# The opening of a two-block layer: partial sums on two engines, product passes outermost, weight rounding ahead of the modulation

## Chip, cores and metric

One core of one Trainium2 chip runs the whole program in one launch. The metric is device time in microseconds (us), the median of several executions; the profile is of one execution.

## The reference, cut to what matters

Two transformer blocks on 256 tokens of 1024 features, in float32. The change touches only the start of the first block:

```python
c_act = silu(c)                                   # (1, 1024)
mod = (c_act @ w_ada + b_ada).reshape(1, 6, 1024) # w_ada: 1024 x 6144
shift1, scale1 = mod[:, 0], mod[:, 1]             # columns 0 to 2047 of w_ada
u = rms_norm(x, ln1) * (1.0 + scale1) + shift1    # (256, 1024)
proj = u @ w_in                                   # only 1536 columns of it in the opening
```

Behind the opening come the rest of `proj`, the convolution and state-space branches, the first MLP, and the whole second block.

## The kernel before

**Precision.** Each float32 product is made of three fp32r products: operands are split into a rounded high part (ScalarE copies to fp32r) and a low part (what the rounding left, a subtraction), and high x high, high x low and low x high are summed in PSUM. For weights the parts are called `wh` and `wl`, for the activations `uh` and `ul`.

**The opening** (lines 386 to 575) stands in a manual schedule: every engine runs its instructions in the order of the program text. It has four pairs p = 0 to 3, each of two blocks k = 2p, 2p+1 of 128 features. The activations `us` are normalised and transposed but not yet modulated. For each pair:

- `load_a0(p)` brings 2 MB of `w_ada` (four transfers on SP's queue, two halves `a0[p,0]`, `a0[p,1]`); `do_load()` brings one block's 0.75 MB of `w_in` into one of four `raw` buffers, which are free again when the weight's low part has been made.
- `acc0(p, h)` on VectorE multiplies the eight 128-row slices by c and adds them up in `ac0` (one tensor_scalar and seven scalar_tensor_tensor of 512 columns per pair).
- `sum0(p)` sums `ac0` over partitions on TensorE (four matmuls with one moving column, each two instructions in the trace), and VectorE makes the scale and shift columns `gs0` (three small instructions).
- `mod0(k)`: ScalarE modulates the 256 tokens of block k in place (line 494) and rounds them to `uh` (495); VectorE makes `ul` (496).
- `split0(k)`: ScalarE rounds the 1536 weight columns to `wh` (lines 503 and 504); the low part is made in three pieces of 512, two on GpSimd and one on VectorE (line 507).
- `prod0(k, u0, u1)`: 36 matmuls of 256 columns per block (6 output tiles x 2 x 3 passes); the six PSUM tiles `first` gather all eight blocks. The three passes of one weight tile follow each other, so `wl` is wanted by the third matmul.

In the loop over k, half of `acc0(p+1)` stands before each block's products on VectorE; `sum0(p+1)` stands in the middle of the odd block's products, followed by `mod0` and `split0` of the next pair. Before the loop SP issues five small vectors (`rc`: c, c_2, ln1, two pieces of b_ada), the two halves of x, pair 0, two weight blocks, pair 1 and two weight blocks. In the loop it issues pair p+2 in the first two pairs, one weight block for each k, and at k = 4 eleven small vectors (`smalls`).

Behind the opening the order is a planner's; weights come through the same `raw`, `wh` and `wl` buffers (four each), and the six `first` tiles are read out there.

Of the kernel before, what the change touches and what calls it, by code (L numbers as in the profile page):

```python
# [8 lines left out]
F32 = mybir.dt.float32  # L9
F32R = mybir.dt.float32r  # L10
AF = mybir.ActivationFunctionType
ALU = mybir.AluOpType
# [25 lines left out]
def tile_hybrid_blocks(ctx: ExitStack, tc: tile.TileContext, a: dict, out: bass.AP, dbg=None):  # L38
    nc = tc.nc
# [13 lines left out]
    act, dve, pool, pe = nc.scalar.activation, nc.vector, nc.gpsimd, nc.tensor  # L53
# [4 lines left out]
    def aux(name):  # L58
        return ps_aux.tile([128, 512], F32, tag="aux", name=name)

    cur = {}
# [149 lines left out]
    tri3 = const.tile([128, 3, 128], F32, name="tri3")  # L211
# [174 lines left out]
    NS = 6  # L386
    start = ExitStack()
    start.enter_context(tc.manual_schedule())
    ph = phase("start")
    rc = cur["p"].tile([40, 128], F32, tag="rc", name="rc")  # L390
    for i, src in enumerate((a["c"][0], a["c_2"][0], a["ln1"][0], a["b_ada"][0, 0:1024], a["b_ada"][0, 1024:2048])):
        nc.sync.dma_start(rc[8 * i : 8 * i + 8], src.rearrange("(r q) -> r q", q=128))
    x0 = cur["p"].tile([128, 2, D], F32, tag="xtok", name="x0")
    for t in range(2):
        nc.sync.dma_start(x0[:, t, :], a["x"][0, t * 128 : (t + 1) * 128, :])
# [1 line left out]
    a0 = {}  # L397

    def load_a0(p):

        for h in range(2):
# [5 lines left out]
    smalls, later_smalls = [], []  # L407
    r1 = cur["p"].tile([96, 128], F32, tag="r1", name="r1")
    rows = [("ln2", a["ln2"][0], 8), ("ln1g2", a["ln1_g_2"][0], 8), ("ln2g2", a["ln2_g_2"][0], 8),
            ("cw", a["conv_w"][0].rearrange("t c -> (t c)"), 24), ("nw", a["ssm_norm_w"][0], 16), ("cbias", a["ssm_conv_b"][0], 32)]  # L410
    base = 0
    at_row = {}
    for nm, ap, n in rows:
        smalls.append((r1[base : base + n], ap.rearrange("(r q) -> r q", q=128)))
        at_row[nm] = base
        base += n
    r2 = cur["p"].tile([128, 128], F32, tag="r2", name="r2")
    smalls.append((r2, a["ssm_conv_w"][0].rearrange("t c -> (t c)").rearrange("(r q) -> r q", q=128)))
    wdt = const.tile([128, 8, 32], F32, name="wdt")
# [33 lines left out]
    dve.scalar_tensor_tensor(ccol, cth, 1.0, csb[:, :16], op0=ALU.add, op1=ALU.mult)  # L453
    dve.tensor_scalar(ccol, ccol, 0.5, None, op0=ALU.mult)
    ada_c.append(ccol)
    bsc = const.tile([128, 8], F32, name="bsc")
    dve.tensor_scalar(bsc, csb[:, 32:40], 1.0, None, op0=ALU.add)
    lncol, bsh = csb[:, 16:24], csb[:, 24:32]
# [3 lines left out]
    gs0 = const.tile([128, 2, 8], F32, name="gs0")  # L462
    ac0 = {}

    def acc0(p, h):
        v = a0.pop((p, h))
        if h == 0:
            ac0[p] = cur["p"].tile([128, 2, 256], F32, tag="ac0", name="ac0", bufs=2)
        t = ac0[p]
        for ko in range(4):  # L470
            c = ccol[:, 4 * h + ko : 4 * h + ko + 1]
            if h == 0 and ko == 0:
                dve.tensor_scalar(t, v[:, ko], c, None, op0=ALU.mult)
            else:
                dve.scalar_tensor_tensor(t, v[:, ko], c, t, op0=ALU.mult, op1=ALU.add)

    def sum0(p):
        t = ac0.pop(p)
        ps = aux("adaps")
        for s_ in range(2):  # L480
            for j in range(2):
                pe.matmul(ps[:, 2 * s_ + j : 2 * s_ + j + 1], t[:, s_, 128 * j : 128 * j + 128], ones32[:, 0:1],
                          start=True, stop=True)
        ks = slice(2 * p, 2 * p + 2)
        dve.tensor_tensor(gs0[:, 0, ks], ps[:, 0:2], bsh[:, ks], op=ALU.add)
        for j in range(2):
            k = 2 * p + j
            dve.scalar_tensor_tensor(gs0[:, 1, k : k + 1], ps[:, 2 + j : 3 + j], bsc[:, k : k + 1], lncol[:, k : k + 1],
                                     op0=ALU.add, op1=ALU.mult)

    def mod0(k):
        p, j = k // 2, k % 2
        f = us[p][:, j, :]
        act(f, f, AF.Identity, scale=gs0[:, 1, k : k + 1], bias=gs0[:, 0, k : k + 1])
        act(uh[p][:, j, :], f, AF.Copy)
        dve.tensor_tensor(ul[p][:, j, :], f, uh[p][:, j, :].bitcast(F32), op=ALU.subtract)

    def split0(k):

        v = raws.pop(k)  # L500
        wh, wl = (w_p.tile([128, 2048], F32R, tag=n_, name=n_, bufs=4)[:, :1536].rearrange("p (k n) -> p k n", k=3)
                  for n_ in ("wh", "wl"))
        act(wh[:, 0:1, :], v[:, 0:1, :], AF.Copy)
        act(wh[:, 1:3, :], v[:, 1:3, :], AF.Copy)  # L504
        for q in (1, 2, 0):
            e_ = dve if q == 2 else pool
            e_.tensor_tensor(wl[:, q, :], v[:, q, :], wh[:, q, :].bitcast(F32), op=ALU.subtract)  # L507
        splits[k] = (wh, wl)
        st["split"] += 1

    def prod0(k, u0, u1):
        wh, wl = splits[k]
        p, jj = k // 2, k % 2
        xh, xl = uh[p][:, jj, :], ul[p][:, jj, :]
        for u in range(u0, u1):
            sec, c0 = (1, 2, 0)[u % 3], 256 * (u // 3)
            for j in range(2):
                ah, al = (w[:, sec, c0 + 128 * j : c0 + 128 * j + 128] for w in (wh, wl))
                for n, (l_, r_) in enumerate(((ah, xh), (ah, xl), (al, xh))):
                    pe.matmul(first[u][:, j, :], l_, r_, start=(k == 0 and j == 0 and n == 0),  # L520
                              stop=(k == 7 and j == 1 and n == 2), skip_group_check=True)

    us = [pair("xt") for _ in range(4)]
    uh = [pair("uh", F32R) for _ in range(4)]
# [17 lines left out]
    for k in range(8):  # L542
        p, odd = k // 2, k % 2
        if not odd and p < 2:
            load_a0(p + 2)
        if k < 4:
            do_load()
        elif k == 4:
            for dst, src in smalls:
                nc.sync.dma_start(dst, src)  # L550
        if k >= 4:
            do_load()
# [12 lines left out]
    pr = aux("pr1")  # L565
    pe.transpose(pr[:, :96], r1, ident[:96, :96])
    pe.transpose(pr[:, 128:256], r2, ident)
# [964 lines left out]
```

## Time and profile before

| | us |
|---|---|
| median of 3 runs (lowest, highest) | 958.37 (956.73, 960.18) |
| profiled execution, time | 957.05 |
| its span, first to last instruction | 955.1 |
| TensorE busy in the span | 906.7 (95%) |
| VectorE busy | 721.5 (76%) |
| ScalarE busy | 498.3 (52%) |
| GpSimd busy | 101.4 (11%) |

In the page's forty slices TensorE is at nine tenths or more nearly everywhere; the first three slices, some 72 us, are at 3, 8 and 8 tenths. A busy TensorE is not TensorE at its peak: ends of matmuls are modelled, and the granted clock has two levels. The pace (start to start) of like instructions tells more than their durations.

### The profile page before, as it was taken

To read this page: it belongs to the slowest core of one execution; us is meant where nothing else is said; L and a number is where in the kernel's file an instruction comes from. 1 tells how busy PE (TensorE), PEld (TensorE's weight loads), DVE (VectorE), ACT (ScalarE), POOL (GpSimd) and SP (SyncE) were. 2 spreads that over 40 slices of the span, in tenths; PEclk is the share of its full clock that TensorE was granted. 3 is DMA by queue.
4 is the path that set the end of the run, shared out by engine and by line. 5 is a ranking of instruction groups with operands and counts; after the bars stand their busy time and mean duration, and the time that the engine had idled before them with its cause. 6 is when DMAs were issued, how large, how long until landed. Compare 5 with 4: busy or idle time off the path is not lost.

```text
span 955.1 us, 15625 instructions
## 1 busy us (share of the span) xinstructions
PE 906.7 (95%) x6320; PEld 827.5 (87%) x6320; DVE 721.5 (76%) x1026; ACT 498.3 (52%) x843; POOL 101.4 (11%) x109
## 2 busy tenths in 40 slices
PE   3889999999999999999999999989899899999997
PEld 2779999999999999979899898867676699999996
DVE  4868979899989997578689698687788585455553
ACT  4246484577676754446444445374566473344430
POOL 5432000110001000100000100023120000000001
PEclk9979999999999999999999999989999999999999
DMA  8948899677875775644879699425443265555511
GB/s 312 334 123 265 288 346 337 223 263 256 295 243 184 260 248 191 220 178 154 309 283 372 228 349 364 168 101 189 151 137 128 89 221 177 186 180 200 184 46 44
DMA packets 124347, 210.77 MB, mean 221 GB/s; under 512 B 5580, under 2 KB 96044, under 8 KB 119028
## 3 DMA queue, kind: packets, MB, share of 16 engines
q1 hardware_dynamic: 121780, 202.18, 61.3%
q0 software_dynamic: 2496, 7.61, 2.3%
q8 instruction: 49, 0.80, 0.3%
q14 instruction: 22, 0.18, 0.1%
HBM read 208.67 MB, written 1.11 MB: 220 GB/s over the span
## 4 chain that ended last, share of the span: by engine, by line
PE 45%; DVE 5%; ACT 2%; POOL 1%; issue 1%; DMA 1%; DVEq 0%; ACTq 0%
PE tmacc L921 17%; PE up L618 15%; PE gate L618 6%; POOL qkr L223 1%; PE fv L1189 1%; DVE wl L130 1%; PE gu L1102 1%; PE up L1102 1%; PE fk L1189 1%; PE dv L1189 1%; PE lg L1286 1%; DMA gate<-gscr 1%; PE fq L1189 1%; ACT f L1016 0%; DVE qn L1264 0%
## 5 line engine op out<-in xcount | busy, mean ns | idle before, releaser
L130 DVE TENSOR_TENSOR wl<-raw,wh 128x1024 fp32r<-128x1024 f32 x264 | 317.5, 1227 | 89.7 <-ACT wh L122 89.6
L122 ACT ACTIVATE wh<-raw 128x1024 fp32r<-128x1024 f32 x264 | 267.1, 1051 | 218.6 <-issue 90.5
L272 DVE SCALAR_TENSOR_TENSOR adaacc<-raw,ccol,adaacc 128x1024 f32<-128x1024 f32 x80 | 99.3, 1279 | 5.0 <-DMA raw<-in_w_ada_dram 5.0
L921 PE MATMUL tmacc<-wh,hidh 128*128 128x512 f32 x216 | 67.2, 392 | 0.0
L921 PE MATMUL tmacc<-wl,hidh 128*128 128x512 f32 x216 | 66.8, 390 | 0.0
L921 PE MATMUL tmacc<-wh,hidl 128*128 128x512 f32 x216 | 66.6, 390 | 0.0
L618 PE MATMUL up<-fh,wh 128*128 128x256 f32 x384 | 54.2, 284 | 0.0
L618 PE MATMUL up<-fl,wh 128*128 128x256 f32 x384 | 53.9, 283 | 0.0
L618 PE MATMUL up<-fh,wl 128*128 128x256 f32 x384 | 53.9, 283 | 0.0
L618 PEld LDWEIGHTS up<-fh,wh 128*128 128x128 f32 x384 | 50.1, 191 | 2.5 <-issue 1.7
L618 PEld LDWEIGHTS up<-fh,wl 128*128 128x128 f32 x384 | 49.5, 192 | 0.0
L618 PEld LDWEIGHTS up<-fl,wh 128*128 128x128 f32 x384 | 49.5, 192 | 0.0
L921 PEld LDWEIGHTS tmacc<-wh,hidl 128*128 128x128 f32 x216 | 40.6, 188 | 8.6
L921 PEld LDWEIGHTS tmacc<-wl,hidh 128*128 128x128 f32 x216 | 40.5, 188 | 8.7
L921 PEld LDWEIGHTS tmacc<-wh,hidh 128*128 128x128 f32 x216 | 38.9, 189 | 7.4 <-ACT r L1173 0.8
L734 DVE SCALAR_TENSOR_TENSOR cv<-xc,cwx,cv 128x255 f32<-128x255 f32 (+2 forms) x96 | 39.6, 478 | 0.3 <-ACT cv L729 0.2
L520 PE MATMUL first<-uh,wl 128*128 128x256 f32 x96 | 30.9, 322 | 5.6 <-POOL wl L507 3.3
L842 PE MATMUL ssmacc<-yl,wh 128*128 128x256 f32 x128 | 35.7, 284 | 0.1
L842 PE MATMUL ssmacc<-yh,wl 128*128 128x256 f32 x128 | 35.7, 284 | 0.0
L842 PE MATMUL ssmacc<-yh,wh 128*128 128x256 f32 x128 | 34.3, 288 | 1.1 <-ACT yh L811 1.1
L520 PE MATMUL first<-uh,wh 128*128 128x256 f32 x96 | 30.9, 322 | 3.0 <-ACT wh L504 3.0
L520 PE MATMUL first<-ul,wh 128*128 128x256 f32 x96 | 30.3, 316 | 0.0
(449 smaller groups left out, 2044.3 us busy)
## 6 DMA issues: line engine op xcount, KB each, us to landing
raw<-in_w_in_dram SPq DMA_DIRECT2D x50, 1024.0 KB, 5.2
raw<-in_w_ada_dram SPq DMA_DIRECT2D x40, 1024.0 KB, 5.0
raw<-in_w_up_dram SPq DMA_DIRECT2D x27, 1024.0 KB, 6.2
raw<-in_w_down_dram SPq DMA_DIRECT2D x27, 1024.0 KB, 4.8
raw<-in_w_gate_dram SPq DMA_DIRECT2D x11, 1024.0 KB, 4.9
a<-in_w_ada_dram SPq DMA_DIRECT2D x16, 512.0 KB, 10.2
raw<-in_w_ssm_out_dram SPq DMA_DIRECT2D x8, 1024.0 KB, 5.1
raw<-in_w_in_dram SPq DMA_DIRECT2D x8, 768.0 KB, 4.5
```

The lines of the kernel that those rows point to most:

```text
L122: act(wh[:, sl, :], v[:, sl, :], AF.Copy)
L130: e_.tensor_tensor(wl[:, sl, :], v[:, sl, :], wh[:, sl, :].bitcast(F32), op=ALU.subtract)
L223: pool.tensor_tensor(rs, ms, nhalf[:, :n], op=ALU.pow)
L272: dve.scalar_tensor_tensor(t[:, sl], v[:, 0, sl], ada_c[-1][:, 8 * blk + k : 8 * blk + k + 1], t[:, sl], op0=ALU.mult, op1=ALU.add)
L520: pe.matmul(first[u][:, j, :], l_, r_, start=(k == 0 and j == 0 and n == 0), stop=(k == 7 and j == 1 and n == 2), skip_group_check=True)
L618: pe.matmul(ps[:, j, :], ww[:, k, j * 128 : (j + 1) * 128], xx(k), start=(k == 0 and n == 0), stop=(k == nk - 1 and n == 2))
L734: dve.scalar_tensor_tensor(v[:, j, d:], ps[:, j, : S - d], wc, v[:, j, d:], op0=ALU.mult, op1=ALU.add)
L842: pe.matmul(ssm_acc[q][:, j, :], l_, r_, start=(i == 0 and j == 0 and k == 0 and n == 0), stop=(i == 7 and j == 1 and k == 1 and n == 2), ...
L921: pe.matmul(accs[t][c], l_, ww[:, kk, c * 512 : (c + 1) * 512], start=(first and kk == 0 and n == 0), stop=(last and kk == 1 and n == 2))
L1102: pe.matmul(ps[:, i * 256 : (i + 1) * 256], l_, ww[:, k, :], start=(i == 0 and k == 0 and n == 0), stop=(i == 1 and k == 7 and n == 2), sk ...
L1189: pe.matmul(ps[t], l_, ww[:, k, :], start=(kk == 0 and n == 0), stop=(kk == 7 and n == 2))
L1286: pe.matmul(pss[e][:, i, :], q[sl, p0 + i, qt * 128 : (qt + 1) * 128], k[sl, p0 + i, 0:w], start=True, stop=True)
```

## The change

- The five small `rc` vectors are issued from ScalarE's queue instead of SP's.
- `acc0` multiplies only slices 0 to 4 (`KP = 5`) on VectorE. The new `part0(p)` lets TensorE do slices 5 to 7: three matmuls with c repeated over 32 columns (`crep`) and one with ones over `ac0`, each into its own 32 of the 128 PSUM partitions (four column groups), 512 columns each. ScalarE copies the 128 x 512 result to `rows`, and `sum0` sums the four groups with four matmuls against `sel` (ones at partitions 0, 32, 64, 96).
- `warm(n)`: n float32 matmuls of 256 columns whose result is overwritten; two before `sum0(0)`, four after it.
- `prod0(k, n)` does one pass over all six tiles (12 matmuls), so the passes are outermost.
- `split0` becomes `high_w` (ScalarE) and `low_w` (all on VectorE, pieces of 1024 and 512; none on GpSimd). `high_w` of the next even block stands ahead of `mod0` on ScalarE. The low part of the activations becomes `low0`.
- The loop runs over pairs; SP's loads are issued two weight blocks at a time, the small vectors in two parts.

```diff
-        nc.sync.dma_start(rc[8 * i : 8 * i + 8], src.rearrange("(r q) -> r q", q=128))
+        nc.scalar.dma_start(rc[8 * i : 8 * i + 8], src.rearrange("(r q) -> r q", q=128))
...
+    crep = cur["p"].tile([128, 3, 32], F32, tag="crep", name="crep")
+    dve.tensor_copy(crep, ccol[:, 5:8].unsqueeze(2).to_broadcast([128, 3, 32]))
+    sel = cur["p"].tile([128, 1], F32, tag="sel", name="sel")
+    pool.memset(sel, 0.0)
+    for g in range(4):
+        pool.memset(sel[32 * g : 32 * g + 1], 1.0)
...
+    KP = 5
+
     def acc0(p, h):
-        v = a0.pop((p, h))
+
+        v = a0[p, h]
         if h == 0:
             ac0[p] = cur["p"].tile([128, 2, 256], F32, tag="ac0", name="ac0", bufs=2)
         t = ac0[p]
-        for ko in range(4):
-            c = ccol[:, 4 * h + ko : 4 * h + ko + 1]
-            if h == 0 and ko == 0:
-                dve.tensor_scalar(t, v[:, ko], c, None, op0=ALU.mult)
+        for ko in range(4 * h, min(4 * h + 4, KP)):
+            if ko == 0:
+                dve.tensor_scalar(t, v[:, ko], ccol[:, 0:1], None, op0=ALU.mult)
             else:
-                dve.scalar_tensor_tensor(t, v[:, ko], c, t, op0=ALU.mult, op1=ALU.add)
+                dve.scalar_tensor_tensor(t, v[:, ko % 4], ccol[:, ko : ko + 1], t, op0=ALU.mult, op1=ALU.add)
 
+    def part0(p):
+
+        a0.pop((p, 0))
+        v, t = a0.pop((p, 1)), ac0.pop(p)
+        ps = aux("adaps")
+        for g in range(4):
+            l_, r_ = (crep[:, g, :], v[:, KP + g - 4]) if g < 3 else (ones32, t)
+            pe.matmul(ps[32 * g : 32 * g + 32, :], l_, r_.rearrange("p s c -> p (s c)"), start=True, stop=True)
+        rows = cur["p"].tile([128, 512], F32, tag="part", name="part", bufs=1)
+        act(rows, ps, AF.Copy)
+        ac0[p] = rows
 
     def sum0(p):
-        t = ac0.pop(p)
-        ps = aux("adaps")
-        for s_ in range(2):
-            for j in range(2):
-                pe.matmul(ps[:, 2 * s_ + j : 2 * s_ + j + 1], t[:, s_, 128 * j : 128 * j + 128], ones32[:, 0:1],
-                          start=True, stop=True)
+        rows = ac0.pop(p)
+        ps = aux("adacs")
+        for i in range(4):
+            pe.matmul(ps[:, i : i + 1], rows[:, 128 * i : 128 * i + 128], sel, start=True, stop=True)
...
-        dve.tensor_tensor(ul[p][:, j, :], f, uh[p][:, j, :].bitcast(F32), op=ALU.subtract)
-
-    def split0(k):
-
+
+    def low0(k):
+        p, j = k // 2, k % 2
+        dve.tensor_tensor(ul[p][:, j, :], us[p][:, j, :], uh[p][:, j, :].bitcast(F32), op=ALU.subtract)
+
+    def high_w(k):
         v = raws.pop(k)
...
-        act(wh[:, 0:1, :], v[:, 0:1, :], AF.Copy)
-        act(wh[:, 1:3, :], v[:, 1:3, :], AF.Copy)
-        for q in (1, 2, 0):
-            e_ = dve if q == 2 else pool
-            e_.tensor_tensor(wl[:, q, :], v[:, q, :], wh[:, q, :].bitcast(F32), op=ALU.subtract)
+        for sl in (slice(1, 3), slice(0, 1)):
+            act(wh[:, sl, :], v[:, sl, :], AF.Copy)
+        splits[k] = (wh, wl, v)
+
+    def low_w(k):
+        wh, wl, v = splits[k]
+        for sl in (slice(1, 3), slice(0, 1)):
+            dve.tensor_tensor(wl[:, sl, :], v[:, sl, :], wh[:, sl, :].bitcast(F32), op=ALU.subtract)
...
+    def warm(n):
+
+        for _ in range(n):
+            pe.matmul(first[NS - 1].rearrange("p a b -> p (a b)")[:, :256], ident, tri3.rearrange("p a b -> p (a b)")[:, :256],
+                      start=True, stop=True)
+
+    def prod0(k, n):
+
         wh, wl = splits[k]
...
+        w, r_ = ((wh, uh), (wh, ul), (wl, uh))[n]
+        for u in range(NS):
...
+    part0(0)
+    warm(2)
     sum0(0)
+    warm(4)
+    high_w(0)
     mod0(0)
-    split0(0)
     mod0(1)
...
+    high_w(1)
+    low0(0)
+    low_w(0)
+    low0(1)
+    for p in range(4):
+        k = 2 * p
+        if p < 2:
             load_a0(p + 2)
...
         if p < 3:
-            acc0(p + 1, odd)
-        if not odd:
-            split0(k + 1)
-        prod0(k, 0, 3)
-        if odd and p < 3:
+            acc0(p + 1, 0)
+            acc0(p + 1, 1)
+        low_w(k + 1)
+        for n in range(3):
+            prod0(k, n)
+        splits.pop(k)
+        if p < 3:
+            part0(p + 1)
+            prod0(k + 1, 0)
             sum0(p + 1)
-            mod0(k + 1)
-            split0(k + 1)
+            high_w(k + 2)
             mod0(k + 2)
-        prod0(k, 3, NS)
-        splits.pop(k)
+            mod0(k + 3)
+            high_w(k + 3)
+            low0(k + 2)
+            low_w(k + 2)
+            low0(k + 3)
+            prod0(k + 1, 1)
+        else:
+            prod0(k + 1, 0)
+            prod0(k + 1, 1)
+        prod0(k + 1, 2)
+        splits.pop(k + 1)
```

## Rows read from the trace of the kernel before

**Rows 1.** Windows (stretch, length, busy us of each engine, granted clock, DMA share, GB/s).

```profile
0.00:80.00 80.00, 54.38 (x352) 50.96 (x355) 52.56 (x74) 29.32 (x53) 39.18 (x47) 0.91 0.75 255
80.00:613.00 533.00, 529.33 (x3983) 497.62 (x3976) 452.79 (x597) 306.52 (x486) 30.97 (x34) 1.00 0.76 264
```

**Rows 2.** Timeline of TensorE: first and last product of the opening (start, duration).

```profile
21.62 0.58 PE L520 MATMUL first<-uh,wh 128*128 128x256 f32 x1 [2.99 <-ACT wh L504]
...
78.92 0.28 PE L520 MATMUL first<-uh,wl 128*128 128x256 f32 x1
```

**Rows 3.** Timeline of VectorE: scale and shift of first and last pair.

```profile
18.67 0.16 DVE L485 TENSOR_TENSOR gs<-adaps,csb 128x2 f32<-128x2 f32 x1 [2.02 <-PE adaps L482]
...
65.73 0.16 DVE L485 TENSOR_TENSOR gs<-adaps,csb 128x2 f32<-128x2 f32 x1 [1.21 <-PE adaps L482]
```

**Rows 4.** Windows of two us in the opening, columns as in rows 1.

```profile
26.00:28.00 2.00, 2.00 (x11) 2.00 (x11) 1.96 (x2) 0.00 (x0) 1.94 (x2) 1.00 1.06 388
...
44.00:46.00 2.00, 0.78 (x7) 0.64 (x6) 1.97 (x3) 0.00 (x0) 0.00 (x0) 1.00 0.05 17
...
50.00:52.00 2.00, 2.00 (x11) 2.00 (x11) 0.76 (x4) 1.39 (x3) 0.00 (x0) 0.50 0.44 69
...
58.00:60.00 2.00, 2.00 (x19) 2.00 (x19) 1.97 (x2) 0.00 (x0) 1.57 (x1) 1.00 1.03 336
```

**Rows 5.** Timeline: VectorE's accumulation and low parts, GpSimd's low part beside them.

```profile
10.65 0.48 DVE L473 TENSOR_SCALAR ac<-a,ccol 128x512 f32<-128x512 f32 x1
...
11.17 5.48 DVE L475 SCALAR_TENSOR_TENSOR ac<-a,ccol,ac 128x512 f32<-128x512 f32 x7
...
20.13 0.42 DVE L496 TENSOR_TENSOR ul<-xt,uh 128x256 fp32r<-128x256 f32 x1 [1.05 <-ACT uh L495]
...
21.65 6.29 POOL L507 TENSOR_TENSOR wl<-raw,wh 128x512 fp32r<-128x512 f32 x4 [7.24 <-ACT wh L504]
...
25.16 4.12 DVE L475 SCALAR_TENSOR_TENSOR ac<-a,ccol,ac 128x512 f32<-128x512 f32 x3
...
29.19 0.68 DVE L507 TENSOR_TENSOR wl<-raw,wh 128x512 fp32r<-128x512 f32 x1
...
29.80 3.11 DVE L475 SCALAR_TENSOR_TENSOR ac<-a,ccol,ac 128x512 f32<-128x512 f32 x4
...
79.89 1.22 DVE L130 TENSOR_TENSOR wl<-raw,wh 128x1024 fp32r<-128x1024 f32 x1
```

**Rows 6.** Timeline: SP's first issues.

```profile
0.81 0.73 SPq L392 DMA_DIRECT2D rc<-in_c_dram  x2
...
2.60 0.83 SPq L395 DMA_DIRECT2D x<-in_x_dram  x2
```

**Rows 7.** Timeline of ScalarE: modulation, rounding, a PSUM row copy.

```profile
19.05 0.60 ACT L494 ACTIVATE xt<-xt,gs 128x256 f32<-128x256 f32 x1 [4.93 <-DVE gs L488]
19.69 0.42 ACT L495 ACTIVATE uh<-xt 128x256 fp32r<-128x256 f32 x1
20.01 0.61 ACT L503 ACTIVATE wh<-raw 128x512 fp32r<-128x512 f32 x1
20.53 1.04 ACT L504 ACTIVATE wh<-raw 128x1024 fp32r<-128x1024 f32 x1
...
188.91 0.59 ACT L245 ACTIVATE adarows<-adaps 128x512 f32<-128x512 f32 x1
```

**Rows 8.** Timeline of TensorE: partition sums, float32 matmuls, a visit in column groups.

```profile
16.79 1.84 PE L482 MATMUL adaps<-ones,ac 128*128 128x1 f32 x8 [3.36 <-DVE ac L475]
...
33.05 1.02 PE L482 MATMUL adaps<-ones,ac 128*128 128x1 f32 x8 [1.05 <-DVE ac L475]
...
180.66 0.38 PE L743 MATMUL scps<-C,B 128*128 128x256 f32 x1
180.87 0.38 PE L744 MATMUL scps<-C,B 128*128 128x128 f32 x2
...
187.37 1.06 PE L285 MATMUL adaps<-adaacc,ones 128*32 128x512 f32 x8
```

More of the change, by code (lines that the diff above doesn't have):

```diff
@@ L416, in tile_hybrid_blocks @@
         base += n
+    N_ROWS = len(smalls) + 1
     r2 = cur["p"].tile([128, 128], F32, tag="r2", name="r2")
@@ L502, in split0 @@
                   for n_ in ("wh", "wl"))
-        act(wh[:, 0:1, :], v[:, 0:1, :], AF.Copy)
-        act(wh[:, 1:3, :], v[:, 1:3, :], AF.Copy)
-        for q in (1, 2, 0):
-            e_ = dve if q == 2 else pool
-            e_.tensor_tensor(wl[:, q, :], v[:, q, :], wh[:, q, :].bitcast(F32), op=ALU.subtract)
+        for sl in (slice(1, 3), slice(0, 1)):
[5 more added lines that the diff above has]
+            dve.tensor_tensor(wl[:, sl, :], v[:, sl, :], wh[:, sl, :].bitcast(F32), op=ALU.subtract)
         splits[k] = (wh, wl)
         st["split"] += 1
-    def prod0(k, u0, u1):
+    def warm(n):
[3 more added lines that the diff above has]
+    def prod0(k, n):
         wh, wl = splits[k]
         p, jj = k // 2, k % 2
-        xh, xl = uh[p][:, jj, :], ul[p][:, jj, :]
-        for u in range(u0, u1):
+        w, r_ = ((wh, uh), (wh, ul), (wl, uh))[n]
+        for u in range(NS):
             sec, c0 = (1, 2, 0)[u % 3], 256 * (u // 3)
             for j in range(2):
[L518 to L521, printed above, removed]
+                pe.matmul(first[u][:, j, :], w[:, sec, c0 + 128 * j : c0 + 128 * j + 128], r_[p][:, jj, :],
+                          start=(k == 0 and j == 0 and n == 0), stop=(k == 7 and j == 1 and n == 2), skip_group_check=True)
     us = [pair("xt") for _ in range(4)]
@@ L537, in tile_hybrid_blocks @@
                 act(us[2 * kq + p][:, :, t * 128 : (t + 1) * 128], ps[:, 2 * p : 2 * p + 2, :], AF.Copy)
+    part0(0)
+    warm(2)
     sum0(0)
+    warm(4)
+    high_w(0)
     mod0(0)
-    split0(0)
     mod0(1)
-    for k in range(8):
-        p, odd = k // 2, k % 2
-        if not odd and p < 2:
+    high_w(1)
[5 more added lines that the diff above has]
+        if p < 2:
             load_a0(p + 2)
-        if k < 4:
             do_load()
-        elif k == 4:
-            for dst, src in smalls:
-                nc.sync.dma_start(dst, src)
-        if k >= 4:
-            do_load()
-        if p < 3:
-            acc0(p + 1, odd)
-        if not odd:
-            split0(k + 1)
-        prod0(k, 0, 3)
-        if odd and p < 3:
+            do_load()
+        elif p == 2:
+            for _ in range(2):
+                do_load()
+            for dst, src in smalls[:N_ROWS]:
+                nc.sync.dma_start(dst, src)
+        else:
+            for dst, src in smalls[N_ROWS:]:
+                nc.sync.dma_start(dst, src)
+            for _ in range(2):
+                do_load()
+        if p < 3:
+            acc0(p + 1, 0)
[7 more added lines that the diff above has]
+            prod0(k + 1, 0)
             sum0(p + 1)
-            mod0(k + 1)
-            split0(k + 1)
+            high_w(k + 2)
             mod0(k + 2)
-        prod0(k, 3, NS)
-        splits.pop(k)
+            mod0(k + 3)
[4 more added lines that the diff above has]
+            prod0(k + 1, 1)
+        else:
+            prod0(k + 1, 0)
+            prod0(k + 1, 1)
+        prod0(k + 1, 2)
+        splits.pop(k + 1)
     pr = aux("pr1")
```

## The prediction

> **What bounds the kernel now.** Read the windows by stage first. From 80 to 613 us TensorE is busy 529.33 of 533 us, in the first 80 us only 54.38 [rows 1]. So behind the opening there is next to nothing to win, and time that the opening gives up should reach the end one for one: what follows is a queue of products that waits for nobody. Next, the timeline of TensorE: the opening's first product starts at 21.62 us, its last at 78.92 [rows 2]. It holds 288 products. In windows at full level 19 start in 2 us, in slow ones 11 [rows 4]; with the exact starts that is 0.12 and 0.213 us each. So the products need 34.6 us at full level and take 57.3. The windows also show that the granted clock reads 0.50 at 50 us (1.2 of 2.4 GHz) and 1.00 at 58. At 26 us it reads 1.00 while the pace is the slow one; I believe the pace.
>
> Then what the pairs wait for. The scale of the first pair is made at 18.67, that of the last at 65.73 [rows 3]: three steps of 15.7 us, where 72 products at full level are 8.6. The timeline of VectorE shows why: with GpSimd's low parts beside them, three accumulations take 4.12 us; without, four take 3.11 [rows 5], so 1.37 against 0.78 each. All of a pair's accumulation must be done before its sum, and TensorE waits for it (1.05 us before the second pair's sum, 3.36 before the first's [rows 8]).
>
> Last, DMA. The 15.7 MB of the opening (x 1.05, w_ada 8.39, w_in 6.29) at 388 GB/s are 40.5 us; at 44 us the engines are nearly empty [rows 4]. So data comes ahead of use now; it must be checked against a shorter opening.
>
> **The head.** (a) SP issues x at 2.60, behind five small vectors that begin at 0.81 [rows 6]. Without them x and all that follows it go 1.8 us earlier at most, 0 at least if the small vectors, or ScalarE which now issues them, come later. I take 1.6, since VectorE's accumulation follows x's norm, and the small vectors are not wanted before it. (b) Three scalar_tensor_tensor fewer in the first sum: seven took 5.48 us [rows 5], so 3 x 0.78 = 2.3. The accumulation ended at 16.65 (11.17 + 5.48); now 16.65 - 1.6 - 2.3 = 12.7. (c) The new visit: eight instructions in four column groups took 1.06 us at the full level [rows 8], so 1.06 to about 2.1. Three of four matmuls do not wait for VectorE; behind the accumulation I count 0.9. (d) ScalarE's copy, 0.59 like the one at 188.91 [rows 7], and a wait, 0.2. Beside it stand two warm matmuls: two float32 instructions of 256 columns each, one every 0.21 us [rows 8], so 0.85 in all at full level, 1.7 at the slow one. I take 1.3. (e) The sum itself, 1.84 at the slow level as before [rows 8]. Scale ready to be made at 12.7 + 0.9 + 1.3 + 1.8 = 16.7, against 18.67. (f) From there to rounded activations 20.11 - 18.67 = 1.44 [rows 3, 7]; weight rounding, which stood behind them until 21.57 (20.53 + 1.04 [rows 7]), is done earlier. On TensorE the four warm matmuls take 1.7 (full) to 3.4 (slow): between 1.5 and 3.4, I take 2.4. First product at 19.1 instead of 21.62, between 18.2 and 20.2.
>
> **The first pair.** VectorE from 18.2: low activations 0.42, low weights 1.22 + 0.68 = 1.9, low activations 0.42, then the next accumulation 0.48 + 4 x 0.78 = 3.6 [rows 5]: done at 24.5. Its data is there: 6.8 MB at 388 GB/s are 17.6 us; 40.5 us of transfers that end near 44.5 began near 4, so now near 2.4, and that makes 20. TensorE: 36 products, 4.3 us at full level, 7.7 slow, to 23.4 or 26.8; the visit's last matmul waits for 24.5 in the first case. With a visit of 1.06, 12 products (1.44) and a sum of 1.0, the second pair's sum ends between 27.5 and 30.3. Before, its scale came after the sum that ran from 33.05 to 34.07 [rows 8]. I take 28.0, near the low end: TensorE runs from the visit on without the stops of 1 to 3 us, and products behind an unbroken run went at the full pace before [rows 4].
>
> **The steady step.** Two loops run between one sum's end and the next.
> - TensorE alone: 72 x 0.12 + 1.06 + 1.0 = 10.7.
> - The round through all engines: scale and shift 0.45, modulation and rounding 1.06 [rows 7], low activations 0.42, low weights 1.9, low activations 0.42, accumulation 3.6, tail of the visit 0.5, 12 products 1.44 (they cover the row copy, 0.8), sum 1.0: 10.8.
>
> They are equal, so small waits of each show. I take 10.9, with 10.7 and 12.5 as bounds (12.5: every VectorE term a quarter longer). Weight rounding (1.04 + 0.61) lies on ScalarE between the row copy and the modulation, beside the 12 products and the sum: hidden; without that cover it would cost up to 1.65 a pair. GpSimd's 26 us of low parts go away; VectorE takes them over and still has less to do, since it loses 12 accumulations and all the contention.
>
> **The end.** Sum of the last pair at 28.0 + 2 x 10.9 = 49.8. Behind it 24 products (2.9) and two blocks of 36 (8.6): last product at 61.3 instead of 78.92, so 17.6 us less.
>
> **Queues.** SP issues pair p+2 and two weight blocks together; a weight load waits until `low_w` has freed its buffer, and pair 3 stands behind block 5, which waits for `low_w(1)` behind an accumulation (about 26.4). By then some 9.4 MB have come of 11.3 issued, so DMA has work for 5 us: no gap. Pair 2 lands near 29.4 (10.5 MB), wanted at about 32; pair 3 near 39, wanted near 43; the last blocks near 43, wanted near 48. The small vectors' eleven issues stand behind blocks 8 and 9 now, and blocks 10 and 11 behind the last of them, about 55: six us before the end, no later than before in relation to it. On ScalarE the five new issues precede the table load and the first activation; what waits behind them is the first norm, which waits for x anyway.
>
> **A page against it.** The visit switches the array from one column group to four and back; the 1.06 us of rows 8 hold at least the way in. The Trainium skill (TensorEngine Tiling, Key Properties) says that a change of tiling mode drains TensorE. If the way back is not in the row, an estimate of a drain is a product's stay less its pace, 0.28 - 0.12 = 0.16 us: two switches in three later pairs make 1 us, and the time would be 941.5. I stay with the row.
>
> **The sum.** The profiled execution took 957.05 for a span of 955.1: 957.05 - 17.6 = 939.5. The median of the runs lies 1.3 above that execution: 940.8. Forecast 940.5.
>
> **Rivals.**
> 1. *The clock falls in each pair* (0.15). Visit and sum are thin stretches, and the level was half at 50 us [rows 4] after a stop and a sum. I let it last 4 us a pair, twice the window shown; that is 19 products at 0.093 us lost each, 1.8 a pair, 5.4 for three, and the slower visit and sum 1 more: 947. For it: thin work twice a pair. Against it: 12 products stand between them, and the stops of 1 to 3 us are gone. The Trainium skill (TensorE: Matmul & The Clock Gate, Part 1) holds that half speed is the resting state and sustained activity lifts it; the rise after 26 us agrees. By that rule the six warm matmuls would also spare the first pair its slow products: 27.5 for its sum, and 940 for the time.
> 2. *VectorE sets the step* (0.10). It is then 11.5 to 12.5 instead of 10.9: 1.2 to 3.2 more, and the first pair's accumulation 1 later: 943 to 945. TensorE would wait before `part0`'s last matmul.
> 3. *Part is given back behind the opening* (0.08). There the planner makes another order, and in place of two small tiles early all six `first` tiles are finished in the last pass. TensorE's 3.7 us of idle up to 613 [rows 1] could grow by 3 to 8: 944 to 949.
> 4. *Slower* (0.03): the level stays low through the whole opening. Step 72 x 0.213 + 2.1 + 1.84 = 19.3; from a first product at 20.2, three steps and 72 slow products (15.3) end at 93.4, 14.5 later than before: 971. It decides from about 190 slow products of 288 on (17.6 / 0.093). Against it: the level rose while products followed each other without a stop, as between 26 and 58 us [rows 4].
> 5. *No change* (0.02): data or a hidden wait keeps the step at 15.
>
> **How the numbers follow.** The forecast has 0.62, with a range of its own of 937 to 943: low end with first pair 27.5 and step 10.7 (18.5 less, and another 2 for the first pair's tail and the noise of the runs), high end with 29.5 and 11.3. Measurement can tell about 0.3%, 3 us, from no change. Cases 1 to 3 are all faster by more: 0.62 + 0.33 = 0.95. The range reaches from 936 to 948, to the clock's and the hand-back's cases.
>
> **What the profile will show.** Right: first product near 19, the pair's scale steps near 11, last product near 61, no GpSimd in the opening, accumulations at 0.78 throughout, products at 0.12 from about 22 us on. The forecast fails if the granted clock dips each pair, if TensorE waits for `ac0` in each visit, or if the stretch of 533 us grows.

## The result, and the profile after

The changed kernel takes 942.52 us (median of 4 runs, 942.02 to 943.34), the kernel before 957.61 (4 runs, three of them those of the table before): a ratio of 0.9839 (95% interval 0.9817 to 0.986), 15.1 us less. The forecast was 940.5 (936 to 948). The profiled execution took 942.64 us for a span of 940.9, against 957.05 and 955.1.

Windows of the changed kernel: the opening and the 533 us behind it, and one pair alone (columns as in [rows 1]).

```profile
0.00:65.00 65.00, 53.66 (x396) 45.81 (x397) 40.67 (x73) 33.16 (x59) 14.31 (x36) 1.00 0.89 311
65.00:598.00 533.00, 528.89 (x3977) 496.62 (x3977) 450.00 (x594) 304.70 (x483) 30.95 (x34) 1.00 0.76 265
...
30.00:41.00 11.00, 11.00 (x90) 9.86 (x89) 8.05 (x16) 5.46 (x9) 0.00 (x0) 1.00 1.07 396
```

The long stretch kept its occupancy (528.89 of 533 us busy, before 529.33 [rows 1]), so the gain lies in the opening. In a pair TensorE now reads as busy all the time, at a granted clock of 1.00, and GpSimd has nothing. Next, VectorE's timeline of the changed kernel.

```profile
12.22 0.48 DVE L482 TENSOR_SCALAR ac<-a,ccol 128x512 f32<-128x512 f32 x1
12.74 3.11 DVE L484 SCALAR_TENSOR_TENSOR ac<-a,ccol,ac 128x512 f32<-128x512 f32 x4
18.84 0.16 DVE L504 TENSOR_TENSOR gs<-adacs,csb 128x2 f32<-128x2 f32 x1 [2.98 <-PE adacs L502]
...
29.90 0.16 DVE L504 TENSOR_TENSOR gs<-adacs,csb 128x2 f32<-128x2 f32 x1 [1.81 <-PE adacs L502]
...
34.24 3.11 DVE L484 SCALAR_TENSOR_TENSOR ac<-a,ccol,ac 128x512 f32<-128x512 f32 x4
...
51.90 0.16 DVE L504 TENSOR_TENSOR gs<-adacs,csb 128x2 f32<-128x2 f32 x1 [1.81 <-PE adacs L502]
```

The scales come in steps of 11.0 us instead of 15.7 [rows 3], and four accumulations take 3.11 us. But the first accumulation starts at 12.22, later than before (10.65 [rows 5]), and the first scale is no earlier than before (18.67 [rows 3]). The head of TensorE's timeline, one visit, and the end of the products:

```profile
7.37 0.30 PE L448 MATMUL pcc<-ident,rc 40*128 40x40 f32 x1 [7.37 <-DMA rc<-in_b_ada_dram]
11.17 3.83 PE L564 MATMUL tf<-ident,xn 128*128 128x128 f32 x16 [3.50 <-DVE xn L371]
14.93 1.06 PE L493 MATMUL adaps<-a,crep 128*32 128x512 f32 x6
15.91 1.04 PE L493 MATMUL adaps<-ac,ones 128*32 128x512 f32 x2
16.89 1.13 PE L538 MATMUL first<-tri,ident 128*128 128x256 f32 x4
17.85 0.95 PE L502 MATMUL adacs<-sel,part 128*128 128x1 f32 x8
18.66 1.97 PE L538 MATMUL first<-tri,ident 128*128 128x256 f32 x8
20.33 1.74 PE L549 MATMUL first<-uh,wh 128*128 128x256 f32 x12
...
26.41 1.05 PE L493 MATMUL adaps<-ac,ones 128*32 128x512 f32 x2 [0.47 <-DVE ac L484]
...
35.56 1.60 PE L549 MATMUL first<-uh,wl 128*128 128x256 f32 x12
37.09 0.63 PE L493 MATMUL adaps<-a,crep 128*32 128x512 f32 x3
...
38.38 1.70 PE L549 MATMUL first<-uh,wh 128*128 128x256 f32 x12
39.92 0.94 PE L502 MATMUL adacs<-sel,part 128*128 128x1 f32 x8
40.72 1.68 PE L549 MATMUL first<-ul,wh 128*128 128x256 f32 x12
...
61.88 1.61 PE L549 MATMUL first<-uh,wl 128*128 128x256 f32 x12
63.32 0.25 PE L619 MATMUL pr<-ident,r 96*128 96x96 f32 x1
```

The first product starts at 20.33 instead of 21.62; the last at 61.88 + 11 x 0.12 = 63.2 instead of 78.92 [rows 2], 15.7 us earlier. The span is 14.2 shorter, so 1.5 us are given back behind the opening.

### The profile page after: what moved, and what is told of

Its sections match the earlier page's. It is cut to its first block, busy times and chain, and to the rows that moved or that the text cites. A ratio compares the mean times of both kernels' runs of the same rounds, so it can differ in the third digit from the quotient of the medians.

```text
span 940.9 us, 15693 instructions
## 1 busy us (share of the span) xinstructions
PE 907.6 (96%) x6364; PEld 823.6 (88%) x6364; DVE 706.9 (75%) x1023; ACT 500.3 (53%) x847; POOL 76.5 (8%) x98
## 4 chain that ended last, share of the span: by engine, by line
PE 85%; DVE 9%; ACT 2%; POOL 1%; DMA 1%; issue 1%; ACTq 0%; DVEq 0%
PE tmacc L974 20%; PE up L671 15%; PE gate L671 6%; PE gl L671 5%; PE ssmacc L895 4%; PE z L671 4%; PE xs L671 4%; PE first L549 3%; PE co L671 2%; DVE wl L130 2%; PE B L671 2%; PE C L671 2%; PE cb L671 1%; PE cc L671 1%; PE cx L671 1%; POOL qkr L223 1%
## 5 line engine op out<-in xcount | busy, mean ns | idle before, releaser
L1544 DVE TENSOR_TENSOR hid<-up,sg 128x512 f32<-128x512 f32 x10 | 6.9, 692 | 27.7 <-PE up L671 27.7
L895 PEld LDWEIGHTS ssmacc<-yh,wh 128*128 128x128 f32 x128 | 23.4, 191 | 2.0 <-ACT yh L864 1.5
L895 PEld LDWEIGHTS ssmacc<-yl,wh 128*128 128x128 f32 x128 | 24.5, 192 | 0.3 <-DVE yl L865 0.3
```

Source lines behind the costliest of these rows:

```text
L895: pe.matmul(ssm_acc[q][:, j, :], l_, r_, start=(i == 0 and j == 0 and k == 0 and n == 0), stop=(i == 7 and j == 1 and k == 1 and n == 2), ...
L1544: dve.tensor_tensor(f, ps, sg, op=ALU.mult)
```

## The experiments

The theory at this point: (1) the largest part is that GpSimd no longer works beside VectorE; (2) column groups, and weight rounding ahead of the modulation, each shorten the round by part of a pair's stretch; (3) the small vectors' new queue made the head longer. Rivals: a part is worth nothing since another bound (TensorE, or the data) takes over; or the order of the passes, or the warm matmuls, are what keeps TensorE's level up.

Each of the first eight undoes or adds one thing in the changed kernel, the last three look for a faster head, and one makes a single part of the change in the kernel before. "End" is the start of the transposition `pr` right behind the last product (79.04 before).

| kernel | median us (lowest to highest, runs) | ratio to before (95%) | 1st, 2nd, 4th scale | end |
|---|---|---|---|---|
| changed | 942.52 (942.02–943.34, 4) | 0.9839 (0.9817–0.986) | 18.84, 29.90, 51.90 | 63.32 |
| small vectors on SP | 940.69 (938.98–941.79, 4) | 0.9822 (0.9806–0.9839) | 17.38, 28.86, 50.85 | 62.27 |
| five more small loads ahead of x | 942.08 (1) | – | 17.62, 29.36, 51.36 | 62.78 |
| norm first | 941.03 (940.19–942.37, 4) | 0.9831 (0.9816–0.9846) | 17.70, 28.76, 50.76 | 62.18 |
| no warm matmuls | 942.32 (941.63–944.07, 4) | 0.9846 (0.9831–0.986) | 19.05, 30.10, 52.10 | 63.52 |
| passes innermost | 942.37 (941.13–942.65, 4) | 0.9838 (0.9821–0.9855) | 19.23, 30.28, 52.28 | 63.80 |
| low parts on GpSimd | 948.87 (946.93–949.21, 4) | 0.9904 (0.9885–0.9922) | 18.73, 33.02, 57.08 | 68.51 |
| sums on VectorE alone | 945.86 (944.42–946.16, 4) | 0.9874 (0.9856–0.9891) | 20.66, 32.18, 55.74 | 67.17 |
| weight rounding behind mod0 | 944.8 (943.47–944.98, 4) | 0.9861 (0.9841–0.9881) | 19.97, 31.63, 54.85 | 66.28 |
| before, low parts on VectorE | 954.3 (952.36–955.97, 8) | 0.9965 (0.9953–0.9977) | 18.68, 33.04, 60.84 | 72.96 |
| norm first, fills held back | 940.51 (940.36–942.07, 4) | 0.9824 (0.981–0.9837) | 19.48, 30.53, 52.53 | 63.96 |
| the same, pair 1 loaded earlier | 940.68 (940.22–941.2, 4) | 0.9822 (0.9809–0.9836) | 17.75, 28.82, 50.81 | 62.23 |
| small vectors on SP, pair 1 earlier | 940.58 (940.3–941.09, 5) | 0.9822 (0.9809–0.9836) | 17.35, 28.42, 50.42 | 61.84 |

Two cautions for reading the table. The variants were timed in later sessions than the changed kernel (the kernel before took 957.29 to 957.99 in them), and of its variants only "low parts on GpSimd" has an interval wholly outside that of the changed kernel; smaller differences rest on the ranges of the runs and on the traces. And in the profiles of eight kernels that issue their first loads alike, the small vectors were there at 7.27 to 7.91 us. Where x's norm stands behind them the head moves with them, so half a microsecond in the first scale need not be the edit's work.

### The small vectors' queue

```diff
-        nc.scalar.dma_start(rc[8 * i : 8 * i + 8], src.rearrange("(r q) -> r q", q=128))
+        nc.sync.dma_start(rc[8 * i : 8 * i + 8], src.rearrange("(r q) -> r q", q=128))
```

> The changed kernel with its five small rc vectors back on SP's queue, ahead of x. Theory (the small vectors come late because they share the transfer engines with x and w_ada): they land near 3.9 us again instead of 7.4, ScalarE is free for the first norm when x lands, VectorE's first accumulation starts near 10.7 instead of 12.2; first product near 18.8 instead of 20.3, time near 941.0. Rival (moving them saved its issue time): x and everything behind it goes 1.8 us later, accumulation near 14.0, time near 944.4.

Timelines of TensorE, then ScalarE, of the kernel before; then ScalarE and SP of the changed kernel.

```profile
3.86 0.29 PE L447 MATMUL pcc<-ident,rc 40*128 40x40 f32 x1 [3.86 <-DMA rc<-in_b_ada_dram]
...
6.21 1.06 ACT L349 ACTIVATE junk<-x 128x1024 f32<-128x1024 f32 x1 [1.57 <-DMA x<-in_x_dram]
```

```profile
0.81 0.89 ACTq L392 DMA_DIRECT2D rc<-in_c_dram  x2
...
7.71 0.20 ACT L452 ACTIVATE csb<-pcc 128x40 f32<-128x40 f32 x1 [3.65 <-PE pcc L448]
7.94 0.21 ACT L453 ACTIVATE cth<-csb 128x16 f32<-128x16 f32 x1
8.06 1.04 ACT L349 ACTIVATE junk<-x 128x1024 f32<-128x1024 f32 x1
...
0.81 0.86 SPq L395 DMA_DIRECT2D x<-in_x_dram  x2
```

Both queues issue from 0.81 on, yet the small vectors were there only at 7.37 instead of 3.86. ScalarE runs `csb` ahead of x's squares, so x's squares, which no longer wait for x, wait for the small vectors: 8.06 instead of 6.21. With the vectors back on SP they are there by 3.78, the first accumulation starts at 10.77, and the last product ends 1.05 us earlier.

The next run tells whether ScalarE's queue is slow or the transfers beside it are. It keeps the vectors on ScalarE and puts five more loads of the same size, which nobody uses, on SP ahead of x.

```diff
+    rd = cur["p"].tile([40, 128], F32, tag="rd", name="rd")
+    for i, src in enumerate((a["c"][0], a["c_2"][0], a["ln1"][0], a["b_ada"][0, 0:1024], a["b_ada"][0, 1024:2048])):
+        nc.sync.dma_start(rd[8 * i : 8 * i + 8], src.rearrange("(r q) -> r q", q=128))
     x0 = cur["p"].tile([128, 2, D], F32, tag="xtok", name="x0")
```

> The changed kernel with five further loads of the same small vectors, into a tile that nobody reads, on SP's queue ahead of x; the rc loads stay on ScalarE's queue. Extra transfers only. Theory (sharing with the big transfers): with nothing but small vectors in flight the rc loads land near 4 us, the first accumulation starts near 10.7 as with rc on SP. Rival (ScalarE's queue itself delivers late): they land near 7.4 as now, accumulation at 12.2 or later.

They landed at 4.02, on ScalarE's queue. So the queue is not slow; what delays them, by these two profiles and the run with the vectors on SP, is the megabytes issued at the same moment from SP. The Trainium skill (DMA: Bandwidth & Descriptors, Issuing engines are not separate DMA queues) says that transfers issued by several engines run on the same 16 DMA engines and interleave, and that issuing from several saves only issue time. The 7.37 against 4.02 agrees.

### The norm ahead of the small vectors

```diff
+    n1 = [rstd(norm_stats(x0, t, "n1"), 1, 1.0 / D, "n1") for t in range(2)]
+    xns = [scaled(x0, t, n1[t]) for t in range(2)]
     pc_ = aux("pcc")
```

(the same two lines are taken out behind `ul`)

> The changed kernel with the first norm (squares, rstd, scaling of x) written ahead of the small vectors' transpose and c's activation; queues as in the changed kernel. Theory (the order on ScalarE holds x's norm behind the late small vectors): squares start near 5 us instead of 8.1, the first accumulation near 9.2 instead of 12.2, first product near 17.5, time near 939.6. Rival (data or TensorE hold the head): accumulation or first product no earlier than now, time 942.6.

x's squares start at 4.43 and the accumulation at 9.41, 2.8 us earlier, but the end comes only 1.14 earlier. VectorE and GpSimd in this run:

```profile
9.34 1.96 DVE L466 TENSOR_SCALAR bsc<-csb 128x8 f32<-128x8 f32 x1
9.41 2.16 DVE L484 TENSOR_SCALAR ac<-a,ccol 128x512 f32<-128x512 f32 x1
...
9.42 1.82 POOL L235 MEMSET adaacc<- 128x2048 f32 x1
```

GpSimd's fills now wait for its share of the norm and then lie beside the first accumulation, whose first instruction takes 2.16 us instead of 0.48 (the small one ahead of it 1.96 instead of 0.16). The visit's last matmul waits 1.58 us for the accumulation.

### What TensorE does in between: warm matmuls, order of passes

```diff
-    warm(2)
     sum0(0)
-    warm(4)
```

> The changed kernel without its six warm matmuls. Theory (full level is there from the end of the transposes, near 15 us, ahead of the first warm matmul): products keep the 0.12 us pace, first product within 0.3 us of 20.3, time 942.2 to 942.8. Rival (the warm matmuls hold the level up): with stops of 1 and 2 us around the first sum the level falls, the first pair's 72 products go at 0.213 us, time 945 to 949.

Nothing that the runs can tell (942.32). But the theory was not right in how. TensorE waits in place of the warm matmuls, and in the first pair the level falls, as the rival had it. TensorE's timeline of this run, then a window:

```profile
20.53 2.11 PE L549 MATMUL first<-uh,wh 128*128 128x256 f32 x12 [1.52 <-ACT uh L514]
22.44 2.71 PE L549 MATMUL first<-ul,wh 128*128 128x256 f32 x12
...
26.52 0.63 PE L493 MATMUL adaps<-a,crep 128*32 128x512 f32 x3
```

```profile
23.00:25.00 2.00, 2.00 (x12) 2.00 (x11) 1.91 (x4) 0.00 (x0) 0.00 (x0) 0.51 1.05 404
```

The first 24 products take 4.5 us instead of 3.0. That lies ahead of a wait: in the changed kernel the visit's last matmul stands until 26.41 for VectorE's accumulation, and here the visit begins at 26.52, just as the accumulation ends (26.56). The 0.2 us at the end are no more than the 0.25 by which the small vectors came later (7.62). So the warm matmuls keep the level up in the first pair and gain no time by it.

```diff
-        w, r_ = ((wh, uh), (wh, ul), (wl, uh))[n]
-        for u in range(NS):
+        for u in range(2 * n, 2 * n + 2):
...
+                for m, (w, r_) in enumerate(((wh, uh), (wh, ul), (wl, uh))):
```

> The changed kernel with the three passes of each weight tile following each other again, two tiles in each call. Theory (VectorE is far enough ahead now): the first weight piece's low part is ready 0.2 us after TensorE wants it, step 11.2 to 11.4, time 943.3 to 944.2. Rival (the pass order is what removed TensorE's waits for low weights, some 8 us in the kernel before): time 948 to 950.

Also nothing (942.37). One wait shows, 0.75 us for `wl` in the first pair; the steps stay at 11.0. With the low parts this early on VectorE, the order of the passes is free in this kernel.

### The three parts of the round

```diff
-        for sl in (slice(1, 3), slice(0, 1)):
-            dve.tensor_tensor(wl[:, sl, :], v[:, sl, :], wh[:, sl, :].bitcast(F32), op=ALU.subtract)
+        for q in (1, 2, 0):
+            e_ = dve if q == 2 else pool
+            e_.tensor_tensor(wl[:, q, :], v[:, q, :], wh[:, q, :].bitcast(F32), op=ALU.subtract)
```

> The changed kernel with two of three low-weight pieces on GpSimd again. Theory (GpSimd beside VectorE slows both): accumulations at 1.0 to 1.4 us instead of 0.78, step near 13, time 948 to 951. Rival (with the passes outermost the low weights are wanted 24 products later, so GpSimd's slowness hides): step at most 11.3, time 942.6 to 943.8.

6.3 us more, the dearest part tried. VectorE, GpSimd and TensorE of this run in the first pair:

```profile
22.16 1.56 DVE L482 TENSOR_SCALAR ac<-a,ccol 128x512 f32<-128x512 f32 x1
23.75 4.03 DVE L484 SCALAR_TENSOR_TENSOR ac<-a,ccol,ac 128x512 f32<-128x512 f32 x4
...
22.14 2.73 POOL L532 TENSOR_TENSOR wl<-raw,wh 128x512 fp32r<-128x512 f32 x2 [1.12 <-ACT wh L525]
...
27.84 1.04 PE L493 MATMUL adaps<-ac,ones 128*32 128x512 f32 x2 [2.01 <-DVE ac L484]
28.81 2.67 PE L550 MATMUL first<-uh,wh 128*128 128x256 f32 x12
```

GpSimd stretches VectorE's accumulation (5.6 us instead of 3.6), TensorE waits 2.01 us for it, and behind that stop twelve products take 2.67 us instead of 1.70 (the granted clock was 0.50 from 31 to 35 us). One cause costs twice: the first step is 14.3 us. The two others are 12.1 and 12.0 us, and the accumulation takes 5.5 in each.

```diff
-    KP = 5
+    KP = 8
```

(and `part0` without its matmuls and copy, `sum0` as in the kernel before)

> The changed kernel with all eight slices summed on VectorE again, without the visit in column groups and the row copy; the sum over partitions as in the kernel before. Theory (the visit and the copy cost TensorE nearly what VectorE saves): round of scale 0.45, modulation 1.06, low parts 2.7, accumulation 5.9, sum 0.9: step 11.3 instead of 11.0, head 0.5 later, time 944 to 945. Rival (the split is the main gain): 2.3 us more for each of four accumulations, all of it showing, time near 951.5.

3.3 us more. VectorE needs 2.4 us more for each accumulation, yet the steps, 11.5 to 11.9, are only 0.5 to 0.9 longer, since the visit and the row copy are gone from the round. The head ends later (first scale 20.66, of which 0.4 came with the small vectors, at 7.79), with the sum at the slow pace, 1.84 us for eight instructions. In the third loop TensorE stops:

```profile
42.12 1.65 PE L496 MATMUL adaps<-ones,ac 128*128 128x1 f32 x8 [1.69 <-DVE ac L484]
```

The granted clock was 0.50 behind it, from 44 to 48 us. So the column groups are worth what they take off VectorE less what they cost TensorE and ScalarE: the theory's size, not the rival's.

```diff
-    high_w(0)
     mod0(0)
+    high_w(0)
     mod0(1)
...
-            high_w(k + 2)
             mod0(k + 2)
+            high_w(k + 2)
```

> The changed kernel with the weight rounding of the even block behind the modulation on ScalarE again. Theory (it lay in the round): low weights 1.1 us later, accumulation 0.6 us later than TensorE's visit, step 11.6, first product 1.4 later, time near 945.8. Rival (hidden): time at most 943.1.

2.3 us more, with steps of 11.6 to 11.7: the rounding had lain in the round, as [rows 7] had it (1.65 us), and part of that shows. Not all of the later end is the edit's: the first scale, ahead of everything that the edit moves, comes 1.1 us later in this profile (small vectors at 7.91, the visit at the slow pace). From the first scale to the end it is 46.3 us instead of 44.5, so the trace shows 1.8.

### One part alone in the kernel before

```diff
-            e_ = dve if q == 2 else pool
-            e_.tensor_tensor(wl[:, q, :], v[:, q, :], wh[:, q, :].bitcast(F32), op=ALU.subtract)
+            dve.tensor_tensor(wl[:, q, :], v[:, q, :], wh[:, q, :].bitcast(F32), op=ALU.subtract)
```

> The kernel before with one part of the change alone: all three pieces of the weights' low parts on VectorE, none on GpSimd; order, accumulation and sums are as before. Theory 'GpSimd beside VectorE is the largest part': accumulations take 0.78 us each throughout; the round through VectorE is two more pieces of 0.68 in front of each half of the accumulation, less what the contention took, 14.2 instead of 15.7 a pair, three pairs and the first loop together about 5 us less: 952 to 953. Rival 'it is worth what undoing it cost the changed kernel' (6.3): 951 or less. Rival 'VectorE was the bound, so work moved onto it takes back what the contention gave': no change, 956.5 to 958.5.

3.3 us less, half of what undoing it cost the changed kernel, and less than either figure expected. The round is as the theory had it (steps 14.4, 13.9, 13.9, and the end 6.1 us earlier), but the span of the profiled execution is only 1.2 shorter. That execution (955.67) is near the slow end of its eight; by the medians about half of the 6.1 us reaches the end. TensorE of this run behind the opening:

```profile
164.60 1.21 PE L617 MATMUL gl<-uh,wh 128*128 128x256 f32 x8 [1.01 <-ACT xc L724]
...
171.09 1.22 PE L617 MATMUL z<-uh,wh 128*128 128x256 f32 x8 [0.48 <-ACT xc L724]
...
178.18 0.66 PE L748 MATMUL xtps<-ident,xs 128*128 128x128 f32 x4 [0.41 <-DVE xs L736]
```

The kernel before has none of these waits (its `xtps` starts at 181.09 without one). Here TensorE stands still for 1.9 us in three places, and at `xtps` 2.9 of the 6.1 us are left. Rival 3 of the prediction, the hand-back behind the opening, is real, and in these profiles larger here than in the changed kernel. Why ScalarE's `xc` comes late here was not looked into.

### A faster head

```diff
+    hold = cur["p"].tile([128, 2], F32, tag="hold", name="hold")
+    pool.tensor_copy(hold, gs0[:, 0, 6:8])
     pr = aux("pr1")
```

(with the norm first)

> The changed kernel with x's norm ahead of the small vectors' transpose on ScalarE, as in the run before of that name, and GpSimd's fills and small loads that stood at 7 to 17 us held back to the end of the opening, so that no fill lies beside VectorE's first accumulation (it took 2.16 us there instead of 0.48). Theory 'the head is a chain of engines': the first accumulation stays near 9.4 and the whole sum ends at 13.0, the first scale comes near 16.2 (17.70 with the fill, 18.84 in the changed kernel), and nearly all of it reaches the end: 939 to 940 us. Rival 'the data of pair 1 is the bound behind the first scale': the first scale comes early all the same, but the second pair's accumulation waits for w_ada until about 21.7, the second scale stays near 28.7 and the time near 941, as with the norm alone.

The edit did not do what it was for. GpSimd's timeline:

```profile
9.56 1.82 POOL L235 MEMSET adaacc<- 128x2048 f32 x1
...
52.85 0.18 POOL L619 COPY hold<-gs 128x2 f32<-128x2 f32 x1 [35.65 <-DVE gs L509]
```

The copy was run at 52.85, the fills still ahead of it, and the accumulation's first instruction took 2.16 us as with the norm first. It is the kernel "norm first" once more, and tests neither theory. Its median is low (940.51) although the first scale in the table is late (19.48): the profiled execution, 942.07, is the slowest of the four, and the others took 940.36 to 940.62.

```diff
     do_load()
-    do_load()
     load_a0(1)
     do_load()
     do_load()
+    do_load()
```

(one `do_load` stays ahead of pair 1; the first of the two runs has the edit above as well, the second the small vectors on SP and pair 1 ahead in the same way)

> As the run above, and pair 1 of w_ada is loaded ahead of the second weight block, so that 0.75 MB less lies in front of it (an estimate from 388 GB/s: 2 us). If the data of pair 1 is the bound, its accumulation starts near 20.2 instead of 21.7, the second scale comes near 27.3 and the time falls to about 939.5. If the chain of engines is the bound, the time is that of the run above, or more by what the second weight block's later high part costs (it would arrive near 21 and be rounded until 22.6, its products start near 24.5).

> The changed kernel with the small vectors back on SP and the order of loads above. The small vectors on SP gave 940.69 with a wait of 0.32 us for pair 1's data. If that data was the bound, the accumulation of pair 1 starts 0.3 to 1 us earlier and the time is 940.0 or a little less; if not, 940.7.

Neither moved the time (940.68 and 940.58). With the small vectors on SP, VectorE had waited 0.32 us for pair 1's data at 21.67; now it starts at 21.23 without a wait, and the end is 0.43 earlier, which the medians do not show. With the norm first it starts at 21.63, as without the edit (21.58). So the data is at most half a microsecond behind, and the chain of engines bounds the head. The four variants with several runs whose first scale is more than a microsecond earlier lie at 940.6 to 941.0, faster than both kernels; the runs of the last two do not overlap with the changed kernel's.

## Why the prediction was right, and where it was off

| step of the prediction | forecast | measured |
|---|---|---|
| (a) first accumulation starts | 9.05 (10.65 − 1.6) | 12.22 |
| (b) accumulation shorter by | 2.3 | 2.37 |
| (c) visit behind it | 0.9 | 1.04 |
| (d) row copy, warm matmuls | 1.3 | 0.96 |
| (e) sum, to the scale | 1.84 | 0.99 |
| first scale | 16.7 | 18.84 |
| (f) from there to the first product | 2.4 | 1.49 |
| first product | 19.1 | 20.33 |
| second pair's sum ends | 28.0 | 29.86 |
| steady step | 10.9 | 11.00, 11.00 |
| last product | 61.3 | 63.2 |

**The size and the place were right**: the step of a pair, which makes up most of the gain (15.7 before), is 11.0 against 10.9. That the median came so near has some luck in it, as the next paragraphs show.

**Step (a) failed in its sign.** It counted the 1.8 us of issue saved on SP and bounded the cost at nothing; it noted that the small vectors "are not wanted before" the accumulation and overlooked that `csb` stands ahead of x's squares on ScalarE. Measured: the accumulation starts 1.57 us later than before instead of 1.6 earlier, and about one microsecond of that reaches the end of the products (the run with the vectors on SP), 1.5 where pair 1 is loaded earlier as well (end 61.84).

**Steps (d) to (f) were too dear**, by 2.1 us together, which hid part of (a). The 1.2 of (d) and (e) count: the first scale is 2.1 us late, not 3.2. The 0.9 of (f) brings only the first product nearer, since the first pair's time goes through VectorE: its accumulation ends at 26.35, and the visit's last matmul waits for it until 26.41. The three steps allowed for the slow pace; in the trace, transposes (11.17 to 15.0) run straight into the visit and the sum, at the fast pace, where the kernel before stood still for 3.36 us ahead of its sum [rows 8].

**The step's bound** is the round through all engines, by a narrow margin. TensorE alone needs what the forecast had, 10.7: six groups of twelve products 8.9, the sum 0.8, a visit 1.0. But in the changed kernel the visit takes 1.29 us (37.09 to 38.38), for its last matmul waits for VectorE, whose accumulation ends at 37.35. TensorE's weight loads of the changed kernel, then TensorE of the run with low parts on GpSimd, where one visit found the accumulation done:

```profile
37.40 0.14 PEld L493 LDWEIGHTS adaps<-ac,ones 128*32 128x32 f32 x2 [0.17 <-DVE ac L484]
```

```profile
41.57 0.63 PE L493 MATMUL adaps<-a,crep 128*32 128x512 f32 x3
...
42.57 1.69 PE L550 MATMUL first<-uh,wh 128*128 128x256 f32 x12
```

That visit took 1.00. TensorE's busy time does not show the wait. From scale to scale the round is 3.82 us to the accumulation, 3.63 for it, 1.03 to the next products, 1.54 for twelve of them and 0.98 for the sum: 11.0. The forecast had 10.8; its tail of the visit (0.5) was 0.5 too small, and what stands ahead of the accumulation (4.25) 0.4 too large. The Trainium skill (TensorEngine Tiling, Key Properties) has a change of tiling mode drain TensorE; the prediction put an estimate of 0.33 us a pair on that and stayed with the row. The trace shows 0.09 us more than the pace ahead of a visit (37.00 to 37.09) and at most 0.10 behind it (twelve products in 1.54 instead of 1.44), so staying with the row was right.

**Rivals.** The clock did not fall in the pairs (granted clock 1.00, and twelve products in 1.44 to 1.57 us throughout). VectorE did hold TensorE in each visit, which the prediction named as a sign of failing, but by little: 0.47 us in the first loop and 0.3 in the others, where rival 2 had 0.6 to 1.6 a step. The hand-back (rival 3) came in small. TensorE of the changed kernel behind the opening:

```profile
63.61 1.05 PE L688 MATMUL dtps<-xt,wdt 128*32 128x256 f32 x10
...
70.54 0.63 PE L688 MATMUL dtps<-xt,wdt 128*32 128x256 f32 x6
...
166.57 0.66 PE L802 MATMUL xtps<-ident,xs 128*128 128x128 f32 x4 [0.42 <-DVE xs L790]
```

What ran in one go of 16 before (79.33 to 80.54) is split in two, and `xtps` waits 0.42 us. The lead over the kernel before is 15.7 us at `pr`, 15.2 behind the second `dtps`, 14.5 at `xtps` and 14.2 at the end. The split is there in every variant of the changed kernel; the wait at `xtps` is not: ten of them lose 0.5 us between `pr` and `xtps`, not 1.2, so part of the hand-back belongs to this one execution.

**The sum.** 957.05 − 17.6 = 939.5 was forecast for the profiled execution and 942.64 came: 1.9 us from the later end of the products (first scale 2.1 late, first pair 0.3 shorter than forecast, two steps 0.2 longer, the last stretch 0.2 shorter), and 1.3 given back (1.5 by the spans). The 1.3 added for the scatter of the runs brought the forecast nearer to the median than its terms were: the terms were 3.1 us short for that execution, the forecast 2.0 for the median, and the changed kernel's median does not lie above its profiled execution. That was luck.

**What each part is worth** (median with it undone, less 942.52): low parts off GpSimd 6.3, column groups 3.3, rounding first 2.3 (1.8 in the trace), order of passes and warm matmuls nothing, the small vectors' queue −1.8. That is 10.1 of 15.1 us; the rest belongs to no single part that was tried. A part's worth depends on the others: 6.3 undone here, 3.3 alone in the kernel before. Loop order and the issue order of loads in the pairs were not tried alone.

## What to carry to other kernels

Price an engine that is idle on paper by what it does to its neighbour: the cheap offload to GpSimd was the dearest part of the opening. Before moving a small load to another queue, look what is issued at that same moment and what stands behind its consumer; issue time saved is not arrival time gained. And read a round both ways, engine by engine and through all engines: where the two agree, as 10.7 and 10.8 here, undoing a part that lies on the round shows. A part that shows nothing may still do something, in front of another wait, as the warm matmuls did.

## What the runs showed of the hardware, unexpected

- Small loads issued at 0.81 us landed at 7.37 beside large transfers of another queue, and at 4.02 on the same queue when that other queue had small loads first.
- Beside a fill by GpSimd (1.82 us) two tensor_scalar of VectorE, one behind the other, took 1.96 us (128 x 8) and 2.16 (128 x 512) instead of 0.16 and 0.48.
- A visit of eight float32 instructions in four column groups between products took 1.00 us from its start to the next product where its operands were ready, 1.29 where the last one came 0.26 us after its start.
- Ahead of the first visit's last matmul, TensorE stood still for 1.58 us with the norm first and for 1.59 with pair 1 loaded earlier, and went on at the full level; in the run "norm first, fills held back" it stood still for 1.91 us and went on at half (1.64 us for the last matmul instead of 1.05, first product at 20.96 instead of 19.24). Windows of the latter, then of the run with pair 1 earlier:

```profile
16.00:18.00 2.00, 2.00 (x5) 1.26 (x5) 0.00 (x0) 1.42 (x2) 0.92 (x2) 0.50 1.10 379
```

```profile
16.00:18.00 2.00, 2.00 (x14) 1.83 (x14) 0.24 (x3) 1.97 (x3) 0.84 (x2) 1.00 1.10 378
```

Five instructions against fourteen in the same two microseconds. It is one profile of each, so no more is read from them than that a head with a stop in it can fall either way.
